# Differential attention with both maps of a head in the two partition halves: score products as pairs of 64-row matmuls

## The chip, the core and the metric

The kernel runs on one core of one Trainium2 chip. The metric is device time in microseconds, from the first to the last instruction of one execution. The engines are TensorE (PE; its weight loads stand as PEld), VectorE (DVE), ScalarE (ACT), GpSimd (POOL) and the DMA queues that SyncE (SP) issues to.

## What is computed

An encoder of two layers on 1024 tokens with 1024 features, in float32. Layer 0 (latent and stick-breaking attention) is not touched. Layer 1 is differential attention with 8 heads; each head has two maps (c = 0, 1) of width 64, and the two softmaxes are subtracted:

```python
def layer_diff(h, rel_table, w_in, lq1, lk1, lq2, lk2, subln_g, w_out, lam_init):
    q, k, v, z = jnp.split(h @ w_in, [DIFF_QK, 2 * DIFF_QK, 2 * DIFF_QK + DIFF_WIDTH], axis=-1)
    q = q.reshape(B, S, DIFF_HEADS, 2, DIFF_HEAD_DIM)      # 8 heads, 2 maps, 64
    k = k.reshape(B, S, DIFF_HEADS, 2, DIFF_HEAD_DIM)
    v = v.reshape(B, S, DIFF_HEADS, 2 * DIFF_HEAD_DIM)
    def block(qs, ke):                                     # 128 queries, keys 0..ke
        s = einsum('bqhcd,bkhcd->cbhqk', q[:, qs:ke], k[:, :ke]) * scale + bias
        p = softmax(where(chunk_mask(qs, ke), s, NEG_INF))
        a = p[0] - lam * p[1]
        return einsum('bhqk,bkhd->bqhd', a, v[:, :ke])
```

Behind it come a norm over the 128 features of a head, a gate, the output projection and the final norm.

## The kernel before

**Precision.** Every float32 operand of a product is split in a high part (rounded to 12 bits) and the exact rest, both held as fp32r. A product is high x high + high x low + low x high, three matmuls into one PSUM bank (`mm3`, L172 to L175).

**Dense blocks.** `dense_fm` (L177) makes 128 features of all tokens: for each of the two halves of the tokens 8 x 3 matmuls of 128 rows and 512 columns. The rows of layer 1 lie in the sixteen resident tiles h1h0..7 and h1l0..7. Each head takes four such blocks: `w1[2h]`, `wv1[h]` (values), `w1[16+h]` (the gate) and `w1[2h+1]`.

**Queries and keys.** The block `w1[2h+c]` holds the 64 query columns and the 64 key columns of map c. `qk_dense` (L361) splits the result and then moves halves between partitions by three DMAs of 64 x 1024: it ends with a = [qh; qh], b = [ql; 0] and k = [kh; kl], each of 128 partitions. The b tiles (`zero_lo`, L374) are QB1 = 3 tiles whose lower half is set to zero once. So a score product is two matmuls of 128 rows, a x k (qh kh + qh kl) and b x k (ql kh): L294 in `scores`.

**Blocks of queries.** `diff_weights(i)` (L1019) does block i of 128 queries. `pieces(i)` says which stretches of keys it computes, one bank each: 256 columns for i = 0 and 1, 384 for 2, 512 for 3, 512 + 256 for 4 and 5, 512 + 384 for 6, 512 + 512 for 7. That is 12 pieces for a map: six of 512, two of 384, four of 256 columns. DVE adds the bias and takes the maximum of each piece (L1029), ACT takes the exponential (L1035), DVE subtracts the maps (L1040). Map 0 goes through this, then map 1. The score banks come from a pool of three (`ps_s`).

**Behind the scores.** `transpose_chunk` (L300) transposes the weights on PE, ACT and DVE split them, `pv_chunk` (L320) multiplies by the values.

**What sets the order.** The instructions of each engine are put in one fixed order when the program is built: the builder runs its own model of the engines and takes, at each step, what is ready there. So the dense matmuls of the next head stand between the score matmuls of a head, and after the last head's dense blocks the output projection of the first tokens does. PE works through its order strictly as it stands.

Of the kernel before, what the change touches and what calls it, by code (L numbers as in the profile page):

```python
# [28 lines left out]
ORDER = (4, 0, 5, 1, 6, 2, 7, 3)      # by chunk parity, small beside large  # L29
ORDER_SEQ = (0, 1, 4, 2, 3, 5, 6, 7)  # first half of the tokens first  # L30
# [7 lines left out]
QB1 = 3  # L38
# [34 lines left out]
def kernel(ctx, tc, a, out):  # L73
# [17 lines left out]
    def res(name, dt=F32R):  # L91
        """one of the sixteen 4 KB residents"""
        return rpool.tile([P, S], dt, name=name, tag="res")
# [13 lines left out]
    # scratch in DRAM  # L107
# [19 lines left out]
    # constants  # L127
# [28 lines left out]
    def split(hi, lo, src, eng_hi="act", eng_lo="vec"):  # L156
        """hi = src rounded to 12 bits, lo = src - hi (exact)."""
        if eng_hi == "act":
            nc.scalar.copy(hi, src)  # L159
        else:  # L160
            (nc.vector if eng_hi == "vec" else nc.gpsimd).tensor_copy(hi, src)
        return sub(eng_lo, lo, src, hi.bitcast(F32))
# [14 lines left out]
    def dense_fm(w, rhs, evac, bank=None):  # L177
        """feature-major rows of one block of 128 columns, in two halves of the tokens"""
        wh, wl = (t.rearrange("p (k c) -> p k c", c=P) for t in w)
        nk = len(rhs)  # L180
        for half in range(2):
            ps = (bank or d_bank)()
            sl = slice(half * 512, half * 512 + 512)
            for k in range(nk):
                mm3(ps, wh[:, k, :], wl[:, k, :], rhs[k][0][:, sl], rhs[k][1][:, sl], k == 0, k == nk - 1)
            evac(ps, half, sl)

    def rstd_cols(pool, ss, n, scale, eps, name, extra=None, bufs=2):
        """(scale * ss + eps * extra) ** -0.5 of [P, n] columns"""
# [16 lines left out]
    def row_out(pool, cols, n, dst, bank):  # L206
        """[P, n] columns (query in block, block) to rows of n blocks in DRAM"""
        tr = bank()
        nc.tensor.transpose(tr[0:n, 0:P], cols, identf)
        row = pool.tile([16, P], F32, name="row", tag="row", bufs=2)  # L210
        nc.vector.tensor_copy(row[0:n], tr[0:n, 0:P])
        dma(dst, row[0:n])

    def row_bc(src, n):
        """a row in DRAM, on n partitions"""
# [5 lines left out]
    def cols_bc(dg, cols, bank):  # L221
        """four columns [P, 4] (query in block, block) as rows on every partition, in a bank"""
# [7 lines left out]
    def row_sums(tile_of, nt, bank):  # L230
        """sums over the partitions of tile_of(t), as columns [P, nt]"""
        ps = bank()
        for t in range(nt):
            mm(ps[:, t:t + 1], tile_of(t), ones, start=True, stop=True)  # L234
        return ps[:, 0:nt]
# [10 lines left out]
    def z_evac(z, func, scale):  # L246
        """z * sigmoid(z), or twice that from tanh(z / 2)"""
# [16 lines left out]
    def v_rows(vs, hi, lo, n):  # L264
        """token-major halves of the values in vs; hi(g), lo(g) of four token tiles"""
# [8 lines left out]
    def v_pair(vs, vt):  # L274
        """[vh|vl] of the even head, [vl|vh] of the odd one, of every token tile"""
        v_rows(vs, lambda g: vt[:, 4 * g:4 * g + 4, 0::3, :], lambda g: vt[:, 4 * g:4 * g + 4, 1:3, :], 2)

# [1 line left out]
    def pieces(i):  # L279
        """(first key, keys, computed keys) of the banks of query block i"""  # L280
# [5 lines left out]
    def scores(i, pairs, mask):  # L286
        """pairs of (stationary, moving) summed into the scores of query block i, one bank a piece"""
# [12 lines left out]
    def transpose_chunk(c, pa, pb):  # L300
        """[q, k] weights of query blocks 2c, 2c+1 to tiles [k, (kb 2j+1 | kb 2j), 256 q]"""
# [18 lines left out]
    def pv_chunk(dst, tiles, passes):  # L320
        """dst[dv, 256] = sum over key blocks; passes(kb) -> [(stationary, 0 hi | 1 lo)]"""
# [39 lines left out]
    def qk_dense(w, hT, b_t, bank=None):  # L361
        """[qh;qh], [ql;0], [kh;kl] of one head whose weights are [q | k]"""
# [9 lines left out]
        return a_t, b_t, k_t  # L372

# [10 lines left out]
    def par_view(ap, par, seq=False):  # L384
        """the tokens of chunks par and 2 + par; with seq of chunks 2 par and 2 par + 1"""
# [7 lines left out]
    def col(i, seq=False):  # L393
        """column of query block i when the columns go by chunk parity"""
        return i if seq else (i // 2) % 2 * 4 + i // 4 * 2 + i % 2

    def put_y(layer, blk, par, y, keep, pool, tag_h, tag_l, bufs):
        """split and store the rows of one parity; keep: tiles that stay on chip instead"""
# [13 lines left out]
    def finish_half(pool, pv, par, e, ot, seq=False):  # L412
        """add the two halves ([vh|vl] or [vl|vh]) of a bank holding the chunks of par_view"""
# [7 lines left out]
    def load_wo(layer, half, f2s, alloc, gate, eng):  # L421
        """feature blocks 2 f2, 2 f2 + 1 of one half of the columns, times the gate, split"""
# [34 lines left out]
    def out_half(ys, wo, fs, x_, xr, bank):  # L457
        """x_ = xr + rows of y times columns of wo"""
# [11 lines left out]
    def ada_sweep(pool, src, acc):  # L470
        """acc[p, n] = sum over kk of c[128 kk + p] ada_w[128 kk + p, n] for 2048 columns"""
# [11 lines left out]
    def ada_cols(dst, bias, acc):  # L483
        """sums over the partitions of the 2048 columns of acc, as [P, 16], and the bias"""
# [11 lines left out]
    # =====================================================================  # L496
    # layer 0: modulation, transposed rows, latents
    # =====================================================================
    hT = [(res(f"h0h{k}"), res(f"h0l{k}")) for k in range(KC)]
    with tc.tile_pool(name="a0", bufs=1, reuse_waits="tile") as a0:  # L500
# [10 lines left out]
        # normalised rows  # L511
# [26 lines left out]
        def ada_block(k):  # L538
            """modulation of features 128 k and on, applied to their transposed rows"""
# [18 lines left out]
        # first three blocks, by features as they come  # L558
# [17 lines left out]
        # relative position rows (times 8) of every head, for the skewed read of layer 1  # L576
# [12 lines left out]
        # modulation of layer 1 and both gates, behind the latents  # L589
# [21 lines left out]
        # latent queries, keys: split with their gains; squares for the norms  # L611
# [26 lines left out]
        # rotated shared key, in every quadrant  # L638
# [5 lines left out]
        with tc.issue_after(ready.ins):  # L644
            # rotary tables: quadrants cos | +-sin | cos | +-sin
# [18 lines left out]
            # lambda  # L664
# [43 lines left out]
    # =====================================================================  # L708
    # attention of layer 0: stick-breaking heads
    # =====================================================================  # L710
# [53 lines left out]
    # =====================================================================  # L764
    # latent heads; the stick-breaking rows of the output projection beside them
    # =====================================================================
# [31 lines left out]
    def rows_part(half, wo, fs, src):  # L798
        """part of the output projection: the feature blocks fs of one half of the columns"""
# [17 lines left out]
    def mla_prep(h):  # L817
        """queries of head h; with an even head the keys and values of its pair too"""
# [88 lines left out]
    # =====================================================================  # L907
    # rest of the output projection of layer 0, rows of layer 1
    # =====================================================================
# [40 lines left out]
    # the first half of the tokens, in tiles that the last latent head leaves free  # L950
# [30 lines left out]
    # =====================================================================  # L981
    # layer 1
    # =====================================================================
# [8 lines left out]
    qb = zero_lo(QB1, qkp)  # L992
    nq = 0

    for h in range(8):
        bank = s_bank if h == 0 else d_bank
        comps = []
        for c in range(2):
            comps.append(qk_dense(wprep(a["w1"][2 * h + c]), hT, qb[nq % QB1], bank))
            nq += 1  # L1000
# [8 lines left out]
        # row 16 a + b starts at 127 - 16 a - b, by whole copies of the row a + b steps on  # L1009
# [9 lines left out]
        def diff_weights(i):  # L1019
# [3 lines left out]
            es = (u_tile(i), w_tile(i))  # L1023
            for c in range(2):
                a_t, b_t, k_t = comps[c]
                e_ = es[c]
                got = scores(i, [(a_t, k_t), (b_t, k_t)], None)
                for n, (ps, sl) in enumerate(got):
                    nc.vector.tensor_tensor_reduce(e_[:, sl], ps, tz[:, S - L + sl.start:S - L + sl.stop], op0=ALU.add,  # L1029
                                                   op1=ALU.max, scale=1.0, scalar=-3e38, accum_out=st[:, n:n + 1])  # L1030
                if i < 4:
                    nc.vector.tensor_scalar(st[:, 2 + c:3 + c], st[:, 0:1], -0.125, None, op0=ALU.mult)
                else:
                    nc.vector.tensor_scalar(st[:, 2 + c:3 + c], st[:, 0:1], st[:, 1:2], -0.125, op0=ALU.max, op1=ALU.mult)  # L1034
# [3 lines left out]
            nc.vector.scalar_tensor_tensor(st[:, 6:7], st[:, 5:6], neglam, lst[:, c1:c1 + 1], op0=ALU.mult,  # L1038
                                           op1=ALU.mult)
            nc.vector.scalar_tensor_tensor(es[1][:, :L], es[1][:, :L], st[:, 6:7], es[0][:, :L], op0=ALU.mult, op1=ALU.add)  # L1040
# [41 lines left out]
    # =====================================================================  # L1082
    # output projection of layer 1, final norm
    # =====================================================================
    wo = [load_wo(1, half, range(4), res, load_gate(yp, 1, half), nc.vector) for half in range(2)]
    # the first half of the tokens, in tiles that the last heads leave free
# [41 lines left out]
def _layout(inputs):  # L1128
# [34 lines left out]
    for h in range(8):  # L1163
        for c in range(2):
            o = h * 128 + c * 64
            b1.append(blk(np.concatenate([q[:, o:o + 64], k[:, o:o + 64]], axis=1)))
# [41 lines left out]
```

## Time and profile before

| | |
|---|---|
| median of 3 runs | 1492.39 us (1489.7 to 1494.19) |
| span of the profiled execution | 1489.6 us |
| PE busy (matmuls) | 1394.9 us, 94% |
| DVE, ACT, POOL busy | 956.8, 670.5, 446.2 us |
| heads of layer 1, 865 to 1340 us: PE busy | 474.77 of 475.00 us |
| end of the last head, 1340 to 1400 us: PE busy | 44.73 of 60.00 us |
| 16 DMA engines, mean busy share 865 to 1340 us | 0.32 |

How to read it: the time that a matmul is said to take includes the way through the array, and the next one begins before it is over. What a matmul costs is therefore the distance from its start to the start of the next, 0.23 us for 512 columns where 0.39 us are reported as its duration. PE busy near 100% means that there was no gap between two reported durations; it hides gaps shorter than the overlap, so the starts have to be read.

### The profile page before, as it was taken

The numbers are of one execution on the slowest core, as the hardware profiler recorded it, in microseconds if no ns is written. First come the engines' busy times: TensorE is split into PE (matmuls) and PEld (weight loads), VectorE is DVE, ScalarE is ACT, GpSimd is POOL, SyncE is SP. The second block draws the span as 40 slices with busy tenths as digits, with TensorE's granted clock in tenths as the row PEclk, the third lists the DMA queues.
The fourth block names the chain that finished last, engine by engine and source line by source line (L and its number), as shares of the span: only waits on it lengthen the run. The fifth ranks groups of instructions, "written<-read, shape, count | busy, mean of one in ns | idle before, by whom it ended". The sixth has DMA issues, their size and how long they took to land.

```text
span 1489.6 us, 20993 instructions
## 1 busy us (share of the span) xinstructions
PE 1394.9 (94%) x7328; PEld 1160.7 (78%) x7328; DVE 956.8 (64%) x2155; ACT 670.5 (45%) x1368; POOL 446.2 (30%) x509
## 2 busy tenths in 40 slices
PE   3899999999998899999879899999999999997797
PEld 2777888888886688887767688888888888886686
DVE  7769637667779865576557526665565756567674
ACT  4452145555556653555345324444444535354321
POOL 1534221132427354635133321133121222134100
PEclk9999999999999999999989999999999999999899
DMA  9269522131224166433747131324232324346262
GB/s 375 67 261 382 206 77 75 49 90 50 75 69 186 36 188 213 136 123 100 215 136 268 29 108 48 86 85 114 71 100 64 92 64 114 78 111 179 82 201 93
DMA packets 109640, 189.85 MB, mean 127 GB/s; under 512 B 8736, under 2 KB 70040, under 8 KB 107488
## 3 DMA queue, kind: packets, MB, share of 16 engines
q1 hardware_dynamic: 109536, 188.53, 39.9%
q8 instruction: 58, 0.95, 0.3%
q14 instruction: 46, 0.38, 0.1%
HBM read 131.23 MB, written 39.27 MB: 114 GB/s over the span
## 4 chain that ended last, share of the span: by engine, by line
PE 40%; DVE 5%; DMA 4%; issue 1%; POOL 1%; ACT 1%; SPq 0%; DVEq 0%; ACTq 0%; POOLq 0%
PE psd L173 8%; PE psd L175 8%; PE psd L174 8%; PE sc L294 4%; PE pv L328 3%; PE sc L173 2%; PE sc L174 2%; PE sc L175 2%; DMA y_hi<-yh_d 1%; DMA w_st<-in_wo_dram 1%; PE pv L234 1%; PE tr L308 1%; PE tr L309 1%; PE tr L310 1%; DVE g L1029 1%
## 5 line engine op out<-in xcount | busy, mean ns | idle before, releaser
L154 POOL TENSOR_TENSOR w_lo<-w_st,w_hi 128x1024 fp32r<-128x1024 f32 (+2 forms) x63 | 153.6, 2440 | 370.7 <-ACT w_hi L159 370.4
L154 DVE TENSOR_TENSOR pt_l<-tr,pt_h 128x512 fp32r<-128x512 f32 (+1 forms) x240 | 148.8, 630 | 104.9 <-ACT pt_h L159 97.4
L159 ACT CAST pt_h<-tr 128x512 fp32r<-128x512 f32 (+1 forms) x240 | 126.2, 547 | 147.0 <-PE tr L310 136.1
L175 PE MATMUL psd<-h1h,w_lo 128*128 128x512 f32 x448 | 177.0, 395 | 0.0
L174 PE MATMUL psd<-h1l,w_hi 128*128 128x512 f32 x448 | 176.2, 393 | 0.0
L173 PE MATMUL psd<-h1h,w_hi 128*128 128x512 f32 x448 | 176.1, 393 | 0.0
L294 PE MATMUL sc<-qk_k,qk_a 128*128 128x512 f32 (+2 forms) x288 | 104.8, 369 | 3.6 <-ACT g L747 1.3
L173 PE MATMUL psd<-h0h,w_hi 128*128 128x512 f32 x264 | 106.7, 404 | 0.0
L174 PE MATMUL psd<-h0l,w_hi 128*128 128x512 f32 x264 | 105.6, 400 | 0.0
L175 PE MATMUL psd<-h0h,w_lo 128*128 128x512 f32 x264 | 105.2, 398 | 0.0
L294 PE MATMUL sc<-qk_k,qk_b 128*128 128x512 f32 (+2 forms) x288 | 98.5, 349 | 0.0
L1029 DVE CUSTOM_DVE_ANT_0 g<-sc,tz 128x512 f32<-128x512 f32 (+3 forms) x128 | 72.1, 585 | 40.1 <-PE sc L294 33.7
L159 ACT CAST w_hi<-w_st 128x1024 fp32r<-128x1024 f32 x56 | 58.9, 1052 | 86.4 <-PE sc L174 36.2
L174 PEld LDWEIGHTS psd<-h1l,w_hi 128*128 128x128 f32 x448 | 84.2, 188 | 17.1
L175 PEld LDWEIGHTS psd<-h1h,w_lo 128*128 128x128 f32 x448 | 84.2, 188 | 16.1
L173 PEld LDWEIGHTS psd<-h1h,w_hi 128*128 128x128 f32 x448 | 84.2, 188 | 16.1
L328 PE MATMUL pv<-pt_l,vt 128*128 128x256 f32 x320 | 88.7, 303 | 8.2 <-DVE pt_l L154 7.4
L1035 ACT ACTIVATE g<-g,st 128x640 f32<-128x640 f32 (+3 forms) x64 | 63.4, 990 | 67.8 <-DVE st L1034 63.1
L328 PE MATMUL pv<-pt_h,vt 128*128 128x256 f32 x320 | 89.5, 296 | 3.3 <-POOL pt_h L314 1.7
L749 DVE TENSOR_TENSOR_SCAN g<-g 128x640 f32<-128x640 f32 (+3 forms) x32 | 68.7, 2148 | 14.7 <-ACT g L746 14.6
L328 PEld LDWEIGHTS pv<-pt_l,vt 128*128 128x128 f32 x320 | 62.0, 194 | 12.0 <-issue 4.7
L328 PEld LDWEIGHTS pv<-pt_h,vt 128*128 128x128 f32 x320 | 61.8, 193 | 9.5 <-DVE ot L418 2.7
(469 smaller groups left out, 3743.3 us busy)
## 6 DMA issues: line engine op xcount, KB each, us to landing
w_st<-in_w_dram SPq DMA_DIRECT2D x46, 512.0 KB
ada_st<-in_ada_k_dram SPq DMA_DIRECT2D x8, 1024.0 KB
ada_st<-in_ada_w_dram SPq DMA_DIRECT2D x16, 512.0 KB
ada_st<-in_ada_w_dram SPq DMA_DIRECT2D x8, 1024.0 KB
w_st<-in_wo_dram SPq DMA_DIRECT2D x16, 512.0 KB
yh_d<-yh SPq DMA_DIRECT2D x28, 256.0 KB
yl_d<-yl SPq DMA_DIRECT2D x28, 256.0 KB
w_st<-in_wv_dram SPq DMA_DIRECT2D x12, 512.0 KB
```

Of the source, the lines that this page charges most:

```text
L154: return (nc.vector if eng == "vec" else nc.gpsimd).tensor_tensor(out_, x_, y_, op=ALU.subtract)
L159: nc.scalar.copy(hi, src)
L173: mm(ps, sh, mh, start=start, stop=False)
L174: mm(ps, sh, ml, start=False, stop=False)
L175: mm(ps, sl, mh, start=False, stop=stop)
L234: mm(ps[:, t:t + 1], tile_of(t), ones, start=True, stop=True)
L294: mm(ps[:, :nn], st[:, q], mv[:, lo_:lo_ + nn], start=m == 0, stop=not diag and m == len(pairs) - 1)
L308: nc.tensor.transpose(tr[:, P:256], pb[:, (2 * j + 1) * P:(2 * j + 2) * P], identf)
L328: mm(dst, st, tt[w][:, m * 256:m * 256 + 256], start=j == 0 and m == 0 and x == 0, stop=j == n - 1 and m == 1 and x == len(ps_) - 1)
L749: nc.vector.tensor_tensor_scan(ur, ur, ur, 1.0, op0=ALU.mult, op1=ALU.bypass)
L1029: nc.vector.tensor_tensor_reduce(e_[:, sl], ps, tz[:, S - L + sl.start:S - L + sl.stop], op0=ALU.add, op1=ALU.max, scale=1.0, scalar=-3e38 ...
L1035: nc.scalar.activation(e_[:, :L], e_[:, :L], AF.Exp, scale=0.125, bias=st[:, 2 + c:3 + c], accum_out=lst[:, c1:c1 + 1] if c == 0 else st[: ...
```

## The change

Each head's two blocks `w1[2h]` and `w1[2h+1]` now hold the queries of both maps and the keys of both maps, so map 0 lies in partitions 0 to 63 and map 1 in 64 to 127 of the tiles that `pair_dense` leaves, without any move. A score product of one map is three matmuls of 64 rows (qh kh, qh kl, ql kh), and `pair_scores` writes those of the two maps in turn, to two banks. The b tiles, their zeroing and the three DMAs of each block go; QB1 goes from 3 to 4.

```diff
-QB1 = 3
+QB1 = 4
+    def pair_dense(w, hT, bank=None):
+        h_t = pools["qk"].tile([P, S], F32R, name="qk_a", tag="qk_a")
+        l_t = pools["qk"].tile([P, S], F32R, name="qk_k", tag="qk_k")
+        def evac(ps, half, sl):
+            split(h_t[:, sl], l_t[:, sl], ps, "act", "vec")
+        dense_fm(w, hT, evac, bank)
+        return h_t, l_t
+    def pair_scores(i, q_, k_, lo_, nn):
+        q = slice(i * P, i * P + P)
+        ks = slice(lo_, lo_ + nn)
+        pss = (s_bank(), s_bank())
+        for m, (x, y) in enumerate(((0, 0), (0, 1), (1, 0))):
+            for c in range(2):
+                r = slice(64 * c, 64 * c + 64)
+                mm(pss[c][:, :nn], q_[x][r, q], k_[y][r, ks], start=m == 0, stop=m == 2)
+        return pss
...
-    qb = zero_lo(QB1, qkp)
...
-            comps.append(qk_dense(wprep(a["w1"][2 * h + c]), hT, qb[nq % QB1], bank))
+            qk.append(pair_dense(wprep(a["w1"][2 * h + c]), hT, bank))
...
-            for c in range(2):
-                a_t, b_t, k_t = comps[c]
-                e_ = es[c]
-                got = scores(i, [(a_t, k_t), (b_t, k_t)], None)
-                for n, (ps, sl) in enumerate(got):
+            for n, (lo_, w_, ww_) in enumerate(pieces(i)):
+                sl = slice(lo_, lo_ + w_)
+                for c, ps in enumerate(pair_scores(i, qk[0], qk[1], lo_, ww_)):
...
+            for c in range(2):
+                e_, m_ = es[c], st[:, 6 + 2 * c:8 + 2 * c]
...
-            o = h * 128 + c * 64
-            b1.append(blk(np.concatenate([q[:, o:o + 64], k[:, o:o + 64]], axis=1)))
+        b1 += [blk(m[:, h * 128:h * 128 + 128]) for m in (q, k)]
```

The fixed order of every engine is the same as before up to the first score matmul of layer 1 (PE; the other engines up to the first instructions of layer 1's first head). Three places on PE follow; sc is a score bank, qk_a and qk_k are the high and the low part (of queries or keys), psd a dense bank with h1h/h1l and a weight tile. L294 is the score matmul of before, L392 that of after.

PE of before, head 0: the two pieces of map 1 of query block 4 (sc_8656, sc_8659), then block 0 of map 0 (sc_8672):

```order
L294 MATMUL sc_8656<-qk_k_8564,qk_a_8563 128x512
L294 MATMUL sc_8656<-qk_k_8564,qk_b1_8367 128x512
L294 MATMUL sc_8659<-qk_k_8564,qk_a_8563 128x256
L294 MATMUL sc_8659<-qk_k_8564,qk_b1_8367 128x256
L294 MATMUL sc_8672<-qk_k_8379,qk_a_8378 128x256
L294 MATMUL sc_8672<-qk_k_8379,qk_b0_8366 128x256
L175 MATMUL psd_9104<-h1h2_7909,w_lo_9101 128x512
```

PE of after, the first pair of banks (sc_8634 is map 0, sc_8635 map 1), all but the first product in turn:

```order
L175 MATMUL sc_8583<-h1h7_7919,w_lo_8551 128x512
L392 MATMUL sc_8634<-qk_a_8554,qk_a_8372 128x512
L173 MATMUL psd_9052<-h1h0_7905,w_hi_9046 128x512
L392 MATMUL sc_8635<-qk_a_8554,qk_a_8372 128x512
L392 MATMUL sc_8634<-qk_k_8555,qk_a_8372 128x512
L392 MATMUL sc_8635<-qk_k_8555,qk_a_8372 128x512
L392 MATMUL sc_8634<-qk_a_8554,qk_k_8373 128x512
L392 MATMUL sc_8635<-qk_a_8554,qk_k_8373 128x512
L174 MATMUL psd_9052<-h1l0_7906,w_hi_9046 128x512
```

PE of after a little on, block 0: map 0 (sc_8664) and map 1 (sc_8665), with 22 dense matmuls between them, of which the first two and the last two stand here:

```order
L392 MATMUL sc_8664<-qk_a_8554,qk_a_8372 128x256
L392 MATMUL sc_8664<-qk_k_8555,qk_a_8372 128x256
L392 MATMUL sc_8664<-qk_a_8554,qk_k_8373 128x256
L174 MATMUL psd_9079<-h1l0_7906,w_hi_9046 128x512
L175 MATMUL psd_9079<-h1h0_7905,w_lo_9047 128x512
```

```order
L173 MATMUL psd_9079<-h1h7_7919,w_hi_9046 128x512
L174 MATMUL psd_9079<-h1l7_7920,w_hi_9046 128x512
L392 MATMUL sc_8665<-qk_a_8554,qk_a_8372 128x256
L392 MATMUL sc_8665<-qk_k_8555,qk_a_8372 128x256
L392 MATMUL sc_8665<-qk_a_8554,qk_k_8373 128x256
```

So where a map's product was two neighbours of 128 rows, it is now three of 64 rows; the two maps stand in turn in some places and apart, with 128-row work between them, in others.

## Rows read from the trace of the kernel before

**Rows 1.** The page's first line.

```profile
span 1489.6 us, 20993 instructions
```

**Rows 2.** Two stretches: us, busy of PE, PEld, DVE, ACT, POOL; clock, DMA share, GB/s.

```profile
865.00:1340.00 475.00, 474.77 (x2537) 406.17 (x2536) 278.11 (x849) 213.72 (x431) 111.84 (x115) 1.00 0.32 86
1340.00:1400.00 60.00, 44.73 (x212) 35.57 (x211) 44.78 (x139) 24.73 (x49) 20.66 (x18) 0.86 0.53 161
```

**Rows 3.** Waits of PE from 865 to 1340: us, times, longest (the only one).

```profile
PE sc L294 <- DMA qk_a<-qk_a: 0.2, 1, 0.2
```

**Rows 4.** Waits of PE from 1340 to 1400: us in total, times, longest.

```profile
PE tr L234 <- ACT sq L1068: 5.2, 1, 5.2
...
PE sc L294 <- DMA qk_a<-qk_a: 0.7, 1, 0.7
```

**Rows 5.** Groups of PE by shape, 865 to 1400: count | busy us, mean ns | idle before.

```profile
L294 PE MATMUL sc<-qk_k,qk_a 128*128 128x512 f32 x96 | 40.0, 416 | 1.4 <-DVE st L1029 1.0 <-DMA qk_a<-qk_a 0.2
...
L294 PE MATMUL sc<-qk_k,qk_a 128*128 128x256 f32 x64 | 17.9, 291 | 0.7 <-DMA qk_a<-qk_a 0.7
...
L294 PE MATMUL sc<-qk_k,qk_a 128*128 128x384 f32 x32 | 11.2, 350 | 0.1
```

**Rows 6.** PE in order of time, 900 to 907: start, duration, line, operation.

```profile
900.02 0.39 PE L294 MATMUL sc<-qk_k,qk_a 128*128 128x512 f32 x1
900.25 0.39 PE L294 MATMUL sc<-qk_k,qk_b 128*128 128x512 f32 x1
...
901.18 0.28 PE L294 MATMUL sc<-qk_k,qk_a 128*128 128x256 f32 x1
901.29 0.28 PE L294 MATMUL sc<-qk_k,qk_b 128*128 128x256 f32 x1
...
906.67 0.34 PE L294 MATMUL sc<-qk_k,qk_a 128*128 128x384 f32 x1
906.85 0.34 PE L294 MATMUL sc<-qk_k,qk_b 128*128 128x384 f32 x1
```

**Rows 7.** PE in order of time, transposes at 909 us.

```profile
909.57 0.27 PE L308 MATMUL tr<-identf,g 128*128 128x128 f32 x1
909.68 0.27 PE L309 MATMUL tr<-identf,g 128*128 128x128 f32 x1
```

**Rows 8.** PE in order of time around a 32-row product (L585).

```profile
79.75 0.40 PE L175 MATMUL psd<-h0h,w 128*128 128x512 f32 x1
80.07 0.81 PE L585 MATMUL tr<-oh,tab 32*8 32x384 f32 x2
80.81 0.50 PE L173 MATMUL sc<-h0h,w_hi 128*128 128x512 f32 x1
81.14 0.39 PE L173 MATMUL psd<-h0h,w_hi 128*128 128x512 f32 x1
...
87.19 0.40 PE L175 MATMUL sc<-h0h,w 128*128 128x512 f32 x1
...
88.59 0.40 PE L174 MATMUL sc<-h0l,w 128*128 128x512 f32 x1
```

**Rows 9.** Weight loads (PEld) at the same place.

```profile
79.52 0.19 PEld L175 LDWEIGHTS psd<-h0h,w 128*128 128x128 f32 x1
80.07 0.09 PEld L585 LDWEIGHTS tr<-oh,tab 32*8 32x8 f32 x2 [0.37 <-PE sc L175]
80.81 0.19 PEld L173 LDWEIGHTS sc<-h0h,w_hi 128*128 128x128 f32 x1 [0.65 <-ACT lat_h L621]
```

**Rows 10.** Line L585: durations in ns, least/median/most.

```profile
L585 PEld LDWEIGHTS tr<-oh,tab x6: 80/82/83, 80.1 to 87.5; 32*8 32x8 f32 x6
L585 PE MATMUL tr<-oh,tab x6: 481/482/484, 80.1 to 87.8; 32*8 32x384 f32 x6
```

**Rows 11.** PE in order of time around a 128-row transpose of 8 columns (L209).

```profile
972.18 0.40 PE L174 MATMUL psd<-h1l,w_hi 128*128 128x512 f32 x1
972.41 0.27 PE L209 MATMUL pv<-identf,rf8r 128*8 128x128 f32 x1
```

More of the change, by code (lines that the diff above doesn't have):

```diff
@@ L991 @@
     yp = enter(db, "yp1", 1)
-    qb = zero_lo(QB1, qkp)
-    nq = 0
     for h in range(8):
         bank = s_bank if h == 0 else d_bank
-        comps = []
+        qk = []
         for c in range(2):
-            comps.append(qk_dense(wprep(a["w1"][2 * h + c]), hT, qb[nq % QB1], bank))
-            nq += 1
+            qk.append(pair_dense(wprep(a["w1"][2 * h + c]), hT, bank))
             if c == 0:
@@ L1023, in diff_weights @@
             es = (u_tile(i), w_tile(i))
-            for c in range(2):
-                a_t, b_t, k_t = comps[c]
-                e_ = es[c]
-                got = scores(i, [(a_t, k_t), (b_t, k_t)], None)
-                for n, (ps, sl) in enumerate(got):
-                    nc.vector.tensor_tensor_reduce(e_[:, sl], ps, tz[:, S - L + sl.start:S - L + sl.stop], op0=ALU.add,
-                                                   op1=ALU.max, scale=1.0, scalar=-3e38, accum_out=st[:, n:n + 1])
+            for n, (lo_, w_, ww_) in enumerate(pieces(i)):
+                sl = slice(lo_, lo_ + w_)
+                for c, ps in enumerate(pair_scores(i, qk[0], qk[1], lo_, ww_)):
+                    nc.vector.tensor_tensor_reduce(es[c][:, sl], ps[:, :w_], tz[:, S - L + lo_:S - L + lo_ + w_], op0=ALU.add,
+                                                   op1=ALU.max, scale=1.0, scalar=-3e38, accum_out=st[:, 6 + 2 * c + n:7 + 2 * c + n])
+            for c in range(2):
+                e_, m_ = es[c], st[:, 6 + 2 * c:8 + 2 * c]
                 if i < 4:
-                    nc.vector.tensor_scalar(st[:, 2 + c:3 + c], st[:, 0:1], -0.125, None, op0=ALU.mult)
+                    nc.vector.tensor_scalar(st[:, 2 + c:3 + c], m_[:, 0:1], -0.125, None, op0=ALU.mult)
                 else:
-                    nc.vector.tensor_scalar(st[:, 2 + c:3 + c], st[:, 0:1], st[:, 1:2], -0.125, op0=ALU.max, op1=ALU.mult)
+                    nc.vector.tensor_scalar(st[:, 2 + c:3 + c], m_[:, 0:1], m_[:, 1:2], -0.125, op0=ALU.max, op1=ALU.mult)
                 nc.scalar.activation(e_[:, :L], e_[:, :L], AF.Exp, scale=0.125, bias=st[:, 2 + c:3 + c],
@@ L1037, in diff_weights @@
             nc.vector.reciprocal(st[:, 5:6], st[:, 4:5])
-            nc.vector.scalar_tensor_tensor(st[:, 6:7], st[:, 5:6], neglam, lst[:, c1:c1 + 1], op0=ALU.mult,
+            nc.vector.scalar_tensor_tensor(st[:, 0:1], st[:, 5:6], neglam, lst[:, c1:c1 + 1], op0=ALU.mult,
                                            op1=ALU.mult)
-            nc.vector.scalar_tensor_tensor(es[1][:, :L], es[1][:, :L], st[:, 6:7], es[0][:, :L], op0=ALU.mult, op1=ALU.add)
+            nc.vector.scalar_tensor_tensor(es[1][:, :L], es[1][:, :L], st[:, 0:1], es[0][:, :L], op0=ALU.mult, op1=ALU.add)
             return es[1]
```

## The prediction

> **What bounds the kernel now.** I read the busy table of two stretches first, since the change touches nothing ahead of layer 1 (the order of every engine is the same until then). From 865 to 1340 us, the heads but the end of the last, PE is busy 474.77 of 475.00 us at a granted clock of 1.00, where DVE has 278 and ACT 214 [rows 2]. The list of waits confirms it: PE waits 0.2 us there in all [rows 3]. So in this stretch each us of TensorE's stream is a us of the result, one way or the other, and nothing that becomes shorter on another engine or queue counts. From 1340 to 1400 the last head has no next head beside it: PE is busy 44.73 of 60.00 us [rows 2] and waits for ACT, DVE and DMAs in turn, 5.2 us at the longest [rows 4]. Then I read the starts of the matmuls, not their durations: a score matmul of 512 columns follows the one before at 0.23 us (0.233 in the mean of such pairs of starts), 384 columns at 0.175 (906.67 to 906.85), 256 columns at 0.117 (901.18 to 901.29) [rows 6].
>
> **What goes.** 192 score matmuls of 512 columns, 64 of 384 and 128 of 256: twice the counts of [rows 5], since each a product has its b product behind it. At the prices above that is 44.7 + 11.2 + 15.0 = 70.9 us of PE, nearly all of it inside the full stretch. The 48 DMAs that put the halves in place go too (three for each of 16 blocks), with the zeroing of b. PE waited 0.2 + 0.7 us for them [rows 3, 4], so at most 0.9 us comes back, and I count nothing. QB1 = 4 lets the next head's blocks start earlier; PE has no gap that this could fill.
>
> **What comes: three products of 64 rows for two of 128.** By columns this is half as much again, 288 + 96 + 192 matmuls, 106.4 us, if they go one after the other. If each pair of maps runs at the same time in the two halves of the array, it is 53.2 us. No row of the trace shows two matmuls side by side, so these are the two ends: +35.5 and -17.7 us. I take it that neighbours of opposite halves do overlap: they read different partitions and write different banks, and nothing in the trace that one matmul takes from another (rows of the array, bank, operands) is shared. The Trainium skill, page "TensorE: Matmul & The Clock Gate", section "Packing small matmuls", reports that matmuls in different row groups run concurrently (3.07 times for four of 32 rows); no run here shows it.
>
> But neighbours must be neighbours. The fixed order decides that, and I counted it in the order of after. The 576 matmuls stand in 119 runs, with 128-row work between runs. 49 runs are three matmuls of one map alone, as block 0 in the change section; others are three of one map, then three of the other, where only the middle two overlap. Taking each neighbour of the opposite half as its partner, 280 matmuls form 140 pairs (100 with a 512, 10 with 384, 30 with 256 as the wider) and 296 have no partner (104, 70 and 122). Pairs: 100 x 0.233 + 10 x 0.175 + 30 x 0.117 = 28.6 us. Singles: 104 x 0.233 + 70 x 0.175 + 122 x 0.117 = 50.8 us. Sum 79.4, which is 8.5 us more than the 70.9 that go, although the pairing works. Then the loads: a transposition of 128 columns follows the next at 0.11 us [rows 7] where 128 columns of stream are some 0.06 by the prices above, so a weight load of 128 columns takes about 0.108 us, one at a time. A pair needs two, 0.216, more than the stream of 256 (0.117) or 384 (0.175) columns: 30 x 0.099 + 10 x 0.041 = 3.4 us if the loads of the two halves stay one behind the other, nothing if they don't. I take 8.5 + 3.4 = **+11.9 us** and keep +8.5 as the lower end.
>
> **What comes: going to 64 rows and back.** The trace of before has one place with another number of rows: line L585, 32 rows, three times, two matmuls each. Around it PE loses time. From the start of the 128-row matmul before (79.75) to that of the second after (81.14) are 1.39 us [rows 8]. In it stream two matmuls of 512 columns (0.46) and the two of L585 (0.81 for both less 0.48 for one, so 0.33 each [rows 8, 10], 0.66). 0.27 us are left; the visit at 87.19 gives 1.40 and so 0.28 [rows 8]. Where they go is seen at the loads: a weight load normally stands at the start of the matmul before it (79.52), but the one of L585 comes at 80.07, about 0.09 after the last stream (79.75 + 0.23), and the next at 80.81, 0.08 after L585's last stream [rows 8, 9]. So PE empties first, and the next load is not hidden. It is not the 8 columns: the 128-row transposition of 8 columns starts 0.23 after its neighbour, with nothing lost [rows 11]. In L585 the load on the way in is one of 8 columns, 0.082 us where one of 128 is 0.19 [rows 9, 10]; a 64-row run loads 128, so I add the difference of 0.106: **0.375 us for a visit**. 119 visits x 0.375 = **+44.6 us**. The lower end is nothing, if 64 rows aren't treated as 32 are; the next is 119 x 0.27 = 32.1. I take 0.375, since the 32-row visit is the one row near to it.
>
> The Trainium skill, page "TensorEngine Tiling (Array Packing)", section "Key Properties", says that a change of the tiling mode drains the engine, for any two modes. It names no price; by that rule the lower end of nothing falls away, and [rows 8] agree for 32 rows alone.
>
> **What moves on the other engines.** DVE, ACT and POOL do the same instructions per piece, but now both maps of a piece come before the next piece, so the first exponential of a block waits for one more bias step of DVE. In the full stretch that is hidden by PE's own queue (DVE has 197 us free there). In the last head it lengthens the chain of one block by well under a microsecond, against the 0.9 us of DMA waits that go: nothing, give or take 5 us of the 15.3 that PE idles there [rows 2].
>
> **Sum.** 1489.6 [rows 1] + 11.9 + 44.6 = 1546.1 in the profiled execution. Its span is 2.8 us below the median of the runs (1492.39), so the forecast against the median is **1549 us**, 3.8% slower. With visits at 0.27 and loads in parallel it is 1533; with 5 us of the last head on top, 1554.
>
> **The rivals.**
> - A: the two halves don't run at the same time, and visits cost what they do above. 1492.4 + 35.5 + 44.6 = 1572.5. For it: no row shows an overlap.
> - B: overlap, but going to 64 rows costs nothing like L585. 1492.4 + 11.9 = 1504. It decides for B if a visit is under some 0.05 us. Against it: both visits in [rows 8].
> - C: the change doesn't do what it says: 64-row matmuls are handled like any other, without overlap and without a visit's price. 1492.4 + 35.5 = 1528.
> - D: within a run, the load for the same half waits until the matmul before it is through. Each of the 296 singles then shows its load of 0.108: 1549 + 32 = 1581. Against it: a 128-row load stands at the start of the matmul before it, and both loads of L585 lie at 80.07 to 80.16 while its matmuls last until 80.88 [rows 8, 9]. The Trainium skill's "TensorE: Matmul & The Clock Gate", section "Packing small matmuls", has this rule, that loads overlap matmuls only where the row group differs; these rows disagree with it.
> - E, faster: the last head's idle 15.3 us [rows 2] go wholly, because its scores no longer wait for DMAs and both maps are ready together; loads run in parallel, visits are free: 1492.4 + 8.5 - 15.3 = 1485.6. It needs a visit of less than (15.3 - 8.5 - 4.5)/119 = 0.02 us to be a gain that counts. Against it: only 0.7 of that idle time is for the DMAs that go [rows 4].
>
> **How the numbers follow.** Forecast 0.59, A 0.11, B 0.14, C 0.06, D 0.05, E 0.02, and 0.03 for what I don't see. A difference of less than 0.3% (4.5 us) can't be told from no change. Faster is E: 0.02. Within 0.3% is B with some of the last head's idle time gone: 0.03. Slower: 0.95. The range takes in A at its top, with 5 us of the last head (1578), C, and B down to a visit of 0.05 us (1492.4 + 11.9 + 6, rounded, 1510); B below that, D's upper part and E are left out, a good tenth.
>
> **What would show it.** Right: PE stays full from 865 us on, the last head's end lies 50 to 60 us later; in the order of time, runs in which the maps alternate start in twos, within 0.02 us, and 0.23 apart, runs of one map at 0.23 one by one; ahead of each run's first load and of the first load behind it stand some 0.09 us after the last stream. Wrong: loads for 64 rows that stand a matmul ahead at the edges of a run (B), pairs that start 0.23 apart (A, C), loads inside a run behind the stream (D), PE idle between heads (a wait that I haven't seen).

## The result, and the profile of the changed kernel

The changed kernel takes 1528.16 us (median of 4 runs, 1526.51 to 1530.67) where the kernel before takes 1493.29 us beside it (4 runs, 1489.7 to 1497.34): a ratio of 1.024, with a 95% interval of 1.0214 to 1.0265. A second set of runs on a chip gave 1527.54 against 1488.84, 1.0258 (1.0226 to 1.029). The forecast was 1549, in a range of 1510 to 1578: slower, as said, but by 35 to 39 us and not by 56. The profiled executions have spans of 1489.6 and 1524.7 us, 35.1 apart.

Busy time of the engines of the changed kernel in the two stretches that answer to [rows 2], and behind them PE's waits in the second (columns as in [rows 2] and [rows 4]). In the first stretch the view of waits has no row.

```profile
865.00:1375.00 510.00, 510.00 (x2681) 399.26 (x2679) 270.00 (x850) 211.84 (x429) 113.19 (x118) 0.99 0.19 57
1375.00:1435.00 60.00, 52.77 (x230) 37.63 (x231) 48.43 (x137) 24.11 (x48) 20.08 (x14) 0.83 0.46 148
```

```profile
PE sc L392 <- DVE st L1044: 3.1, 3, 1.5
PE tr L234 <- ACT sq L1085: 2.4, 1, 2.4
PE psd L173 <- DVE xa L483: 1.8, 1, 1.8
```

PE is full through the heads, as it was, and the heads simply last longer. In the last head it idles 60.00 - 52.77 = 7.2 us where it idled 15.3. One more thing differs: the clock in the heads is 0.99 and not 1.00.

**Edges.** PE of the changed kernel in order of time around the first runs of 64-row matmuls (start, duration, line, operation), and then its weight loads there.

```profile
876.16 0.39 PE L174 MATMUL psd<-h1l,w_hi 128*128 128x512 f32 x1
876.48 0.38 PE L392 MATMUL sc<-qk_a 64*128 64x256 f32 x1
876.79 0.50 PE L175 MATMUL psd<-h1h,w_lo 128*128 128x512 f32 x1
877.12 0.40 PE L173 MATMUL psd<-h1h,w_hi 128*128 128x512 f32 x1
877.45 0.38 PE L392 MATMUL sc<-qk_a 64*128 64x256 f32 x1
877.45 0.50 PE L392 MATMUL sc<-qk_k,qk_a 64*128 64x256 f32 x2
877.67 0.39 PE L392 MATMUL sc<-qk_a,qk_k 64*128 64x256 f32 x2
877.79 0.28 PE L392 MATMUL sc<-qk_a 64*128 64x256 f32 x1
877.91 0.28 PE L392 MATMUL sc<-qk_k,qk_a 64*128 64x256 f32 x1
878.03 0.27 PE L392 MATMUL sc<-qk_a,qk_k 64*128 64x256 f32 x1
```

```profile
876.47 0.18 PEld L392 LDWEIGHTS sc<-qk_a 64*128 64x128 f32 x1 [0.35 <-issue]
876.79 0.19 PEld L175 LDWEIGHTS psd<-h1h,w_lo 128*128 128x128 f32 x1
876.89 0.19 PEld L173 LDWEIGHTS psd<-h1h,w_hi 128*128 128x128 f32 x1
877.45 0.18 PEld L392 LDWEIGHTS sc<-qk_a 64*128 64x128 f32 x1 [0.36 <-issue]
877.45 0.29 PEld L392 LDWEIGHTS sc<-qk_k,qk_a 64*128 64x128 f32 x2
877.56 0.30 PEld L392 LDWEIGHTS sc<-qk_a,qk_k 64*128 64x128 f32 x2
877.68 0.19 PEld L392 LDWEIGHTS sc<-qk_a 64*128 64x128 f32 x1
877.80 0.18 PEld L392 LDWEIGHTS sc<-qk_k,qk_a 64*128 64x128 f32 x1
```

A single 64-row matmul of 256 columns between 128-row ones: from 876.16 to 877.12 are 0.96 us, in which two times 512 and once 256 columns stream (0.23 + 0.23 + 0.117). Some 0.38 us are lost. As around the 32-row product of [rows 8, 9], the load into the run comes 0.09 after the last stream (876.16 + 0.23, load at 876.47), and so does the load out of it (876.48 + load and stream, 876.79). Each edge is thus a gap of 0.09 us and a load of some 0.105 us (877.45 to 877.67, less a stream of 0.117) that nothing hides. Measured in this way over the runs of 64-row matmuls, a visit costs **0.395 us** in the median, whatever the pattern of the run (most lie between 0.39 and 0.41).

**Overlap.** Two runs of the changed kernel in order of time. The first was written as three matmuls of one map, then three of the other (its order stands below).

```profile
900.77 0.39 PE L174 MATMUL psd<-h1l,w_hi 128*128 128x512 f32 x1
901.09 0.45 PE L392 MATMUL sc<-qk_a 64*128 64x384 f32 x2
901.37 0.34 PE L392 MATMUL sc<-qk_k,qk_a 64*128 64x384 f32 x2
901.54 0.34 PE L392 MATMUL sc<-qk_a,qk_k 64*128 64x384 f32 x2
901.81 0.50 PE L175 MATMUL psd<-h1h,w_lo 128*128 128x512 f32 x1
...
906.62 0.50 PE L392 MATMUL sc<-qk_a 64*128 64x384 f32 x2
906.90 0.46 PE L392 MATMUL sc<-qk_k,qk_a 64*128 64x384 f32 x2
907.08 0.51 PE L392 MATMUL sc<-qk_a,qk_k 64*128 64x384 f32 x2
907.26 0.39 PE L392 MATMUL sc<-qk_a 64*128 64x512 f32 x1
907.50 0.39 PE L392 MATMUL sc<-qk_k,qk_a 64*128 64x512 f32 x1
907.73 0.38 PE L392 MATMUL sc<-qk_a,qk_k 64*128 64x512 f32 x1
```

```
L392 MATMUL sc<-qk_a 128x384
L392 MATMUL sc<-qk_k,qk_a 128x384
L392 MATMUL sc<-qk_a,qk_k 128x384
L392 MATMUL sc<-qk_a 128x384
L392 MATMUL sc<-qk_k,qk_a 128x384
L392 MATMUL sc<-qk_a,qk_k 128x384
```

Here the first matmuls of both maps start together, at 901.092 and 901.102, and the second and third ones in the same way, though in the program's order the other map's first is the fourth of the run. From 901.09 to 901.81 are 0.72 us: a load, three streams of 0.175 and the gap of 0.09 behind them, not six streams and not the five slots that neighbours would give. So the two halves work as two streams, each in its own order, and a run lasts as long as the fuller half. Adding up, for each of the 119 runs, the columns of either half at the prices of [rows 6] and taking the larger gives **72.2 us** for all scores, where the forecast had 79.4 + 3.4 and the kernel before 70.9. The trace bears the sum out run by run: from the first load to the end of the last stream a run takes its fuller half and one load, to 0.01 us in the median of each of the common patterns. The loads of the two halves run side by side too: two at 877.45, and pairs of 256 columns then follow at 0.12 us.

### The profile page after: what moved, and what is told of

It reads as the page before. It is cut to its first block, busy times and chain, and to the rows that moved or that the text cites. A ratio compares the mean times of both kernels' runs of the same rounds, so it can differ in the third digit from the quotient of the medians.

```text
span 1524.7 us, 21252 instructions
## 1 busy us (share of the span) xinstructions
PE 1440.4 (94%) x7520; PEld 1159.4 (76%) x7520; DVE 950.2 (62%) x2155; ACT 670.2 (44%) x1368; POOL 445.4 (29%) x506
## 3 DMA queue, kind: packets, MB, share of 16 engines
q1 hardware_dynamic: 105696, 175.94, 35.1%
## 4 chain that ended last, share of the span: by engine, by line
PE 78%; DVE 10%; DMA 4%; ACT 3%; issue 2%; POOL 1%; SPq 0%; DVEq 0%; ACTq 0%; POOLq 0%
PE psd L173 15%; PE psd L174 15%; PE psd L175 15%; PE pv L328 7%; PE sc L392 6%; PE sc L294 4%; PE sc L173 3%; PE sc L174 3%; PE sc L175 3%; PE tr L308 1%; PE tr L309 1%; PE tr L310 1%; DVE ack L565 1%; DMA y_hi<-yh_d 1%; PE tr L307 1%
## 5 line engine op out<-in xcount | busy, mean ns | idle before, releaser
L174 PE MATMUL psd<-h1l,w_hi 128*128 128x512 f32 x448 | 181.1, 404 | 0.0
L173 PE MATMUL psd<-h1h,w_hi 128*128 128x512 f32 x448 | 180.4, 403 | 0.0
L1044 DVE CUSTOM_DVE_ANT_0 g<-sc,tz 128x512 f32<-128x512 f32 (+3 forms) x128 | 72.2, 585 | 35.9 <-PE sc L392 32.7
L328 PE MATMUL pv<-pt_h,v_t 128*128 128x256 f32 x320 | 66.2, 283 | 0.0
L392 PE MATMUL sc<-qk_a 64*128 64x512 f32 (+2 forms) x192 | 62.0, 444 | 3.1 <-DVE st L1044 3.1
```

What stands on the lines that cost most here:

```text
L173: mm(ps, sh, mh, start=start, stop=False)
L174: mm(ps, sh, ml, start=False, stop=False)
L328: mm(dst, st, tt[w][:, m * 256:m * 256 + 256], start=j == 0 and m == 0 and x == 0, stop=j == n - 1 and m == 1 and x == len(ps_) - 1)
L392: mm(pss[c][:, :nn], q_[x][r, q], k_[y][r, ks], start=m == 0, stop=m == 2)
L1044: nc.vector.tensor_tensor_reduce(es[c][:, sl], ps[:, :w_], tz[:, S - L + lo_:S - L + lo_ + w_], op0=ALU.add, op1=ALU.max, scale=1.0, scala ...
```

## The experiments

A few numbers of each trace carry most of what follows. The heads' stretch is from the first score matmul to the first matmul of the output projection of layer 1; PE waits for nothing there in any kernel of the table (0.2 us in the one before), so it adds up. With the new layout eleven value products and seven transpositions more fall into it than before, some 2 us of PE, in the kernels with six products for a pair. "Low clock" is the time at which the granted clock is 0.5 in it; PE does half as much in it, so half of it is added time.

| kernel | visits in all / in the stretch | heads' stretch us | low clock us | ratio to before (95%) |
|---|---|---|---|---|
| before | 0 / 0 | 462.0 | 0 | 1 |
| changed | 119 / 103 | 506.3 | 6.8 | 1.024 (1.0214 to 1.0265) |
| changed, again | 119 / 103 | 506.3 | 6.8 | 1.0258 (1.0226 to 1.029) |
| 64 rows in before | 192 / 169 | 537.9 | 23.9 | 1.0501 (1.0471 to 1.0532) |
| same half | 119 / 103 | 539.2 | 10.2 | 1.0533 (1.0513 to 1.0553) |
| full rows | 0 / 0 | 495.0 | 0 | 1.0198 (1.0172 to 1.0225) |
| two products | 0 / 0 | 461.4 | 0 | 0.9982 (0.9966 to 0.9999) |
| maps in order | 109 / 95 | 506.1 | 13.7 | 1.022 (1.0191 to 1.0249) |

The first four kernels below ran on one chip, beside the same runs of the kernel before.

**A visit by itself.** In the kernel before, the b product takes the 64 rows that aren't zero. Nothing else changes: not the order, not the columns, not the DMAs.

```diff
-                got = scores(i, [(a_t, k_t), (b_t, k_t)], None)
+                got = scores(i, [(a_t, k_t), (b_t[0:64], k_t[0:64])], None)
```

> The kernel before with one edit: in layer 1 the second product of each score (b x k, ql times kh) takes only partitions 0 to 63, where the lower half of b is zero anyway. Same columns, same fixed order, no two halves at work together; the 192 matmuls are 192 visits to 64 rows. Theory (a visit costs 0.395 us, as the edges in the trace of after show it): 1493 + 192 x 0.395 = 1569 us. Rival (64 rows are handled like any other and after is slower only by its columns): 1493 us.

1561.46 us against 1488.41, +73.05, or 0.380 us for each of 192 visits, but with the low clock in it and with visits in the last head, where PE has idle time. The heads' stretch is cleaner: 537.9 - 462.0 = 75.9, less 23.9 / 2 for the low clock, over 169 visits: 0.378. The price of a visit is real for 64 rows and doesn't need two maps, new tiles or pairs.

**Overlap taken away, visits left.** The changed kernel with both maps on rows 0 to 63, in the same order of PE.

```diff
-                r = slice(64 * c, 64 * c + 64)
+                r = slice(0, 64)
```

> The kernel after with one edit: both maps take partitions 0 to 63, so map 1 is computed from map 0's rows and the outputs differ. The fixed order of every engine is that of after, with 119 visits, but no two matmuls lie in opposite halves. Theory (in after the two halves run beside each other, each run as long as its longer half, 72.2 us in all): the 106.4 us of all columns come one after the other, 1528 + 34 = 1562 us. Rival (no overlap in after): 1528 us.

1567.89 us, +79.5, 6 us more than the 1562 expected. PE of this kernel in order of time, in a run of alternating maps of 256 columns:

```profile
882.54 0.39 PE L392 MATMUL sc<-qk_a 64*128 64x256 f32 x1
882.77 0.40 PE L392 MATMUL sc<-qk_k,qk_a 64*128 64x256 f32 x2
883.01 0.39 PE L392 MATMUL sc<-qk_a,qk_k 64*128 64x256 f32 x2
883.25 0.28 PE L392 MATMUL sc<-qk_a 64*128 64x256 f32 x1
```

Two matmuls of 256 columns now take 0.24 us, where the two at 877.67 above took 0.12. In the heads' stretch this costs 539.2 - 506.3 = 32.9 us, less 1.7 for the low clock, 31.2. The columns that no longer overlap are 106.4 - 72.2 = 34.2 us for all scores; 513 of the 576 matmuls lie in the stretch, which makes 30. So the overlap is there, and it is worth what the starts say.

**Neither overlap nor visits.** All 128 rows for each of the 576 products, in the same order again. The matmuls have the columns of the changed kernel and no edges.

```diff
-                r = slice(64 * c, 64 * c + 64)
+                r = slice(0, 128)
```

> The kernel after with one edit: the six products of a pair take all 128 partitions (each score then mixes both maps, the outputs differ). Same fixed order, no visit and no overlap. Theory (visits cost 119 x 0.395 = 47 us, overlap gives 34): after - 47 + 34 = 1515 us, and before + 35.5 less what the last head waits less = 1521 to 1529, so 1515 to 1529. Rival (neither visits nor overlap are worth anything): 1528, with edges at 64 rows in after's trace that look like these. Either way the edges of its score runs should show no gap.

1517.43 us, +29.0. PE of this kernel, in order of time, at the first score matmul:

```profile
877.24 0.40 PE L175 MATMUL sc<-h1h,w_lo 128*128 128x512 f32 x1
877.47 0.39 PE L392 MATMUL sc<-qk_a 128*128 128x512 f32 x1
877.70 0.40 PE L173 MATMUL psd<-h1h,w_hi 128*128 128x512 f32 x1
```

No gap on either side. Against the same half, with the same columns one after the other, the heads' stretch is 44.2 us shorter, less 5.1 for the low clock, 39.1 over 103 visits: **0.380 us**, the same as in the first experiment by another way.

**The rest of the change.** The kernel of full rows with two products instead of three: the new tiles, no DMAs between partitions, QB1 = 4, and as many columns as before.

```diff
-        for m, (x, y) in enumerate(((0, 0), (0, 1), (1, 0))):
+        for m, (x, y) in enumerate(((0, 0), (1, 0))):
...
-                r = slice(64 * c, 64 * c + 64)
-                mm(pss[c][:, :nn], q_[x][r, q], k_[y][r, ks], start=m == 0, stop=m == 2)
+                r = slice(0, 128)
+                mm(pss[c][:, :nn], q_[x][r, q], k_[y][r, ks], start=m == 0, stop=m == 1)
```

> The kernel after with the products of e3 and the qh x kl product left out: two of 128 rows for each map, as many columns as before, no visit, none of the 48 DMAs, QB1 = 4, maps in turn (the scores mix both maps and lack one product, the outputs differ). It shows what the layout without the 64-row products is worth. Theory (nothing but the last head's idle time, 0 to -8 us, and at most 0.9 us of DMA waits): 1484 to 1493 us. Rival (the new order of the chain behind the scores costs): above 1495 us.

1485.67 us, 2.7 less than before (0.9982, 0.9966 to 0.9999), and a heads' stretch of 461.4 against 462.0. All that the change saves beside the matmuls is worth nearly nothing, as it was costed. The third product then adds 495.0 - 461.4 = 33.6 us to the stretch; by the columns it is 94.1 - 62.8 = 31.3, and the 18 small matmuls that stand in the one stretch and not in the other (some 2 us) make up most of the rest.

**The changed kernel once more**, unchanged, on the chip of the next two.

> The kernel after once more, beside the next two on one chip. Theory: scores 72.2 us for 70.9 (+1.3), 119 visits at 0.395 (+47.0), up to 8 us less waiting in the last head, some us more at the lower clock in the heads: before + 35 to 45. It also shows whether the 5.7 us by which layer 1 began earlier in the first profile of after comes again (theory: no, it goes with the us at the lower clock in layer 0, whose program is the same).

1527.54 us, +38.7; the stretch is again 506.3. What was expected of the beginning of layer 1 missed: its first matmul starts at 809.2, early again (814.0 before, 808.3 in the first profile of the change), and with more time at the low clock ahead of it, 58.0 us against 47.8 and 41.0. So the early start does not come from the low clock alone.

**All runs paired (three tries).** If the unpaired matmuls were the loss, score tiles of two banks, which let both maps start at once, would have given it back. For two banks a pair, banks had to be taken from other uses. In the three orders all but 2, 18 and 8 of the 576 matmuls have a partner.

```diff
-        pss = (s_bank(), s_bank())
+        pair_ = PS["p"].tile([P, 2, 512], F32, name="sc", tag="sc")
+        pss = (pair_[:, 0, :], pair_[:, 1, :])
...
+    banks(1, p=2, t=NT1, v=1, d=ND1)
```

With p = 2 pairs, NT1 = 2 transposition and ND1 = 1 dense bank (72 visits):

> The kernel after, but in layer 1 the two banks of a pair are one tile of two banks (two such tiles, two transposition banks, one value bank, one dense bank instead of two), so that no map starts before both its banks are free. In the fixed order every score matmul then has its partner, and there are 72 visits instead of 119. Theory (visits are the loss): scores 53.2 us for 70.9 (-17.7), 72 x 0.395 = +28.4: before + 11, more if the single dense bank makes PE wait. Rival (the loss lies in the 64-row products themselves or the chain behind them, visits are cheap): before - 18 to after.

With NT1 = 1 and ND1 = 2 (110 visits):

> As e6, but with two dense banks and one transposition bank: again every matmul has its partner, with 110 visits in the fixed order. Theory: -17.7 + 110 x 0.395 = before + 26, so 15 us slower than e6 with the same products; more if the single transposition bank makes PE wait. Rival (visits are cheap): no slower than e6.

With p = 1, NT1 = 2 and ND1 = 3 (98 visits):

> As e6 and e7 (the two banks of a pair are one tile), but one such tile, two transposition banks, one value bank and three dense banks, so that neither the dense blocks nor the transpositions lack a bank; only the next pair waits for its own tile. In the fixed order every matmul has its partner and there are 98 visits. Theory: -17.7 + 98 x 0.395 = before + 21, some us more at the lower clock, so some 15 us faster than after. Rival (PE waits for the banks whatever the split, as in e6 and e7): after or slower.

They took 1562.75 (1.049, 1.0455 to 1.0526), 1565.52 (1.0499, 1.0456 to 1.0541) and 1554.59 us (1.044, 1.0413 to 1.0466). PE's waits from 860 to 1450 us in the first of them (the three largest of more):

```profile
PE psd L180 <- DVE zt L260: 11.8, 6, 2.2
PE sc L400 <- ACT qk_a L166: 9.8, 12, 1.4
PE tr L315 <- DVE pt_l L161: 6.0, 6, 1.4
```

and PE of the third in order of time:

```profile
955.45 0.40 PE L400 MATMUL sc<-qk_a,qk_k 64*128 64x512 f32 x2
957.26 0.51 PE L400 MATMUL sc<-qk_a 64*128 64x512 f32 x2 [1.41 <-DVE st L1054]
```

All three missed what was expected by 43 to 63 us. The numbers expected rested on a PE that stays full, though waits were named as what could add to them; it doesn't stay full. It is busy 544.60, 562.29 and 556.78 of the 590 us, where the changed kernel has 7 idle. With one dense bank PE waits most for DVE and ACT behind the dense blocks (the first two rows above), with one transposition bank for ACT's split of the transposed weights (7.8 us in five places), and with one pair of score banks for DVE's bias step between two pieces (8.8 us in eight places). They also spend more time at the low clock in these 590 us: 47.8, 64.9 and 41.0 us, where the changed kernel has 27.3. They tell nothing on the price of a visit. They show that longer runs bought with banks from other uses bring waits for banks; whether longer runs without that would pay, no run here shows.

**Neighbours or halves.** The changed kernel with the three products of map 0 written first and then those of map 1. Counted by neighbours this order has fewer pairs (89.7 us of stream where the change has 79.4), counted by halves it has as many (71.9 against 72.2); it has 109 visits.

```diff
-        for m, (x, y) in enumerate(((0, 0), (0, 1), (1, 0))):
-            for c in range(2):
-                r = slice(64 * c, 64 * c + 64)
+        for c in range(2):
+            r = slice(64 * c, 64 * c + 64)
+            for m, (x, y) in enumerate(((0, 0), (0, 1), (1, 0))):
```

> The kernel after with the two loops of pair_scores exchanged: three products of map 0, then three of map 1, to the same banks. In the fixed order there are 109 visits for 119 and few neighbours of opposite halves. Theory (the two halves are two streams of their own; a run takes as long as its longer half): scores 71.9 us for 72.3, ten visits fewer: after - 4. Rival (only neighbours overlap, as the prediction counted): scores 89.7 us for 79.3, ten visits fewer: after + 6.

1523.94 us, +33.7 against the before of its own chip, where the changed kernel had +34.9 and +38.7. In the heads' stretch, 506.1 less 6.8 for the low clock is 499.3; the changed kernel has 506.3 less 3.4, 502.9. That is 3.6 us less; by halves it would be the price of 8 visits, 3 us, less, and by neighbours some 6 more. The ratios to before (1.022 against 1.024 and 1.0258) could not decide it, the stretch does: the order inside a run doesn't matter, it is the halves that count.

None of these kernels beats the one before; the two-product kernel, 0.2% below it, leaves a product out.

## Why the prediction was right, and where its sum was not

**What held.** PE bounds the heads, so its stream alone had to be counted; the moved work of the other engines and the DMAs are worth nothing (two products: -2.7 us). The two maps overlap. A visit to 64 rows costs what the 32-row place let one expect: 0.375 was taken, and the runs give 0.395 (the trace of the change), 0.378 and 0.380 (experiments). The visits are the loss, and they were the largest term: 119 x 0.395 = 47.0 us where 44.6 were forecast. But the range, 1510 to 1578, was wide enough for A and C too, so the time alone bears out little: it is the rows and the experiments that bear out the mechanism. One of the signs named for it missed: the end of the last head (the last score matmul, 1386.98 and 1422.98) lies 36 us later and not 50 to 60.

**The step that failed: "neighbours must be neighbours".** This was assumed and nothing in the trace of before could bear it out. Pairs were counted in the program's order, and the 296 matmuls without a neighbour were costed as singles. The trace of the change shows the halves as two streams (901.09), and the exchanged loops confirm it. The columns then cost 72.2 us and not 79.4. The second part of that term, loads of the two halves one behind the other (+3.4), was nothing, as in the lower end that the prediction kept: two loads start at 877.45. So +11.9 us was really 72.2 - 70.9 = **+1.3**.

**The last head** was put at nothing, give or take 5. From 1340 us on to the end PE idled 24.1 us before (149.00 - 124.94); from 1375 on it now idles 16.4 (149.00 - 132.64). So 7.7 us come back, more than the bound. The waits for ACT's squares are down from 5.2 [rows 4] to 2.4. It isn't the DMAs that go: the two-product kernel still idles 15.1 us in the like 60 us, and the kernel of full rows 13.3. The first experiment shows what it is. It adds nothing but visits to the kernel before, and from the output projection on its PE is busier by the same amount (before, then 64 rows in before):

```profile
1338.00:1489.00 151.00, 126.94 (x616) 103.96 (x614) 95.84 (x324) 43.87 (x95) 21.97 (x23) 0.93 0.44 141
1408.00:1559.00 151.00, 134.47 (x614) 105.33 (x613) 96.22 (x324) 43.65 (x95) 21.46 (x20) 0.93 0.42 137
```

It idles 16.5 us where before idles 24.1, and from the first matmul of the output projection to the end it takes 151.6 us where before takes 151.3, with 23 visits there. So visits in the last head fill time in which PE would have waited, and cost next to nothing. The prediction counted all 119 at the full price; 16 of them lie there.

**The clock** was not in the sum at all. The changed kernel has 6.8 us more at 0.5 in the heads and 6.8 more between the first output projection and the last score: 3.4 us for certain, since PE is full in the heads, and up to 3.4 more.

**Ahead of layer 1** the programs are the same, yet in these two profiles the first matmul of layer 1 starts at 814.01 before and at 808.33 now. Over the kernels of the table that start lies between 808 and 816, so 5.7 us of the difference of the spans are spread between executions and not the change. In the second set the ratio is a little higher.

The terms, us:

| | forecast | measured |
|---|---|---|
| columns, pairing and loads | +11.9 | +1.3 |
| visits | +44.6 | +47.0 |
| clock | 0 | +3.4 to +6.8 |
| last head, idle | 0, give or take 5 | -7.7 |
| ahead of layer 1, these two profiles | 0 | -5.7 |
| sum | +56.5 | +38.3 to +41.7; the spans say +35.1 |

By place the spans close: layer 1 begins 5.7 us earlier, from there to the first score are 1.1 us less, the heads' stretch is 44.3 us longer, and what lies behind it is 2.4 us shorter, 35.1 in all. The account of the stretch by terms is a little high: 103 visits x 0.395 = 40.7 (39.1 at the 0.380 of the experiments), 0.7 for columns, 2.0 for the 18 small matmuls and 3.4 for the clock make 46.8 (45.2). Which term is too large by these 1 to 2.5 us was not settled.

**The rivals.** C gave 1528, the very number measured, and it is wrong: it had neither overlap nor a visit's price, and both are there. The kernel that really is C, full rows, has +29.0 us. That two terms of 35 and 47 us with opposite signs end near one that leaves both out is chance; a time alone could not have told them apart, the starts at 901.09 and the edges at 876.48 do. A (no overlap, visits) is the same-half kernel, +79.5 where A said +80. B (free visits) falls with the first experiment. D falls with the loads at 877.68 and 877.80: they are loads for map 0's half and start with that half's matmul before them, whose starts are 877.67 and 877.79; and the last matmuls of one map at 907.26, 907.50 and 907.73 follow each other at the price of their columns. The Trainium skill's "TensorE: Matmul & The Clock Gate", section "Packing small matmuls", says in its list of what overlaps that loads overlap running matmuls only across row groups; these rows don't agree. E asked for free visits.

The same section of the Trainium skill says that matmuls start strictly in the program's order. The run at 901.09 and the exchanged loops speak against that for the two halves of the array: a fourth matmul starts with the first.

## What to carry to other kernels

Count changes of the number of rows on a full PE before counting columns: each trip from 128 rows to 64 and back cost 0.38 to 0.40 us here, as much as some 850 columns at 0.233 us for 512, and two full halves side by side (34 us) did not pay for 119 of them (47 us). By these prices pairing can be worth it only where many 64-row matmuls stand together; no run here shows a gain. Where longer runs have to be bought with banks that other work uses, waits for banks come instead (three tries, +64 to +77 us). Trips that fall where PE would have waited anyway cost next to nothing, so count only those on a full PE. When something new may overlap, bound it by the two streams being independent as well as by neighbours alone.

## What the hardware showed that was not expected

**Halves start out of the written order**, 0.010 us apart, with the fourth matmul of a run beside the first; their loads run side by side as well (two at 877.45). So the sentence ahead of the prediction that PE works through its order strictly as it stands holds for each half by itself, not for the two together.

**The clock falls inside a full stretch.** From the first score to the output projection the kernel before never leaves 2.4 GHz. The changed kernel is at 1.2 GHz for 3.4 us from 954.0 and again from 1240.7. PE of the changed kernel in order of time there:

```profile
951.30 1.84 PE L234 MATMUL pv<-ones_sq,sq 128*128 128x1 f32 x16
953.07 0.39 PE L392 MATMUL sc<-qk_a 64*128 64x256 f32 x2
...
953.98 0.57 PE L392 MATMUL sc<-qk_a 64*128 64x256 f32 x1
...
954.92 0.79 PE L174 MATMUL psd<-h1l,w_hi 128*128 128x512 f32 x1
955.51 0.63 PE L175 MATMUL psd<-h1h,w_lo 128*128 128x512 f32 x1
955.93 0.63 PE L173 MATMUL psd<-h1h,w_hi 128*128 128x512 f32 x1
```

The matmuls of 512 columns behind it follow at 0.42 to 0.43 us instead of 0.23, though PE counts as busy throughout. Ahead of both falls stand sixteen matmuls of one column (1.8 us) and then 64-row visits. That is no accident of this trace: each of the twelve falls in the heads' stretches of the table begins in such a group of sixteen or at most 2.6 us behind its end. The kernels without visits have the same six groups in their heads and no fall, and not every group with visits behind it has one. In the table, every kernel with visits has time at the low clock in the heads' stretch (6.8 to 23.9 us), and the three without visits have none, full rows with its 576 matmuls among them. So the falls go with both, the groups and the visits; which of the things around them the clock answers to was not taken apart. It makes a visit dearer than its edge.
